# Eleven of the 22 groups of a feed-forward block's down projection by Strassen's seven products, five of them with sums of weights formed earlier and kept in DRAM

## The chip, the cores and the metric

The kernel runs on one core of one Trainium2 chip. The metric is the device time of one execution, in microseconds. Before the change three runs gave 1447.15, 1447.38 and 1447.71 us; the median is 1447.38.

## What is computed

One layer of a streaming encoder over 256 frames of 2048 channels, in float32: two token mixers side by side, their merge, then a feed-forward block with a short convolution on its gate half, and a last RMSNorm. The change lies in the feed-forward block:

```python
D_MODEL = 2048; SEQ = 256; D_FF = 5632; CONV_WIDTH = 3

def conv_glu(h, w_up, conv_w, conv_b, w_down):
    ug = h @ w_up
    gate, up = ug[..., :D_FF], ug[..., D_FF:]
    gate = lax.conv_general_dilated(
        gate, conv_w[:, None, :].astype(gate.dtype), window_strides=(1,),
        padding=((CONV_WIDTH - 1, 0),), dimension_numbers=('NWC', 'WIO', 'NWC'),
        feature_group_count=D_FF) + conv_b
    return (jax.nn.silu(gate) * up) @ w_down

def reference(...):
    ...
    h = h + conv_glu(rmsnorm(h, norm_ffn[l]), w_up[l], conv_w[l], conv_b[l], w_down[l])
    return rmsnorm(h, norm_final)
```

## The kernel before

**Products.** Every operand of a large product is split in two fp32r parts, `hi` (ScalarE copies, L96) and `lo` (VectorE subtracts, L97). `mm3` (L103) makes one product of three matmuls: activations 128 x 128 as the stationary operand, weights of up to 512 columns as the moving one, ah*bh, al*bh and ah*bl.

**Up projection** (loop over j, L910, 44 steps). A step loads two tiles of `w_up`, 1 MB each (`load_split`, L109), splits them, runs 32 matmuls of 512 columns (`wide`, L919) and 32 of 256 (`narrow`, L927), and then VectorE and ScalarE apply the norm, the convolution and SiLU (L940 to L954). The result is stored split in the units `ah` and `al`: as plain operands, or, for groups in `STRASSEN`, as three blocks of activations and four sums of blocks (`sums`, L353).

**Down projection** (`down_pair`, L1079). The 2048 output columns come in two pairs of 512-column blocks, p = 0 and 1 (1024 columns each), one after the other. In each, the 5632 rows of `w_down` are walked in 22 groups of 256 rows: one 1 MB load holds the four 128 x 512 blocks b21, b11, b12, b22 of a group. Four PSUM banks (`final`) collect the results.

- A plain group: two `pieces` of 1024 columns are split; 8 products, 24 matmuls.
- A Strassen group (`seven`, L312, and `strassen`, L330): VectorE forms b12 - b11 and b22 - b12 in `t13`, a unit buffer (L317), then b22 - t1 (L319) and b21 - that (L324); 3 1/2 splits of 1024 columns; 7 products, 21 matmuls. Four of the seven go into four more banks (`shared`), which after the last Strassen group are added to `h` (`h_steps`, L464).

**Order and buffers.** A planner puts each engine's instructions in order from the program's order, dependencies and free buffers. `weights_first` lets loads and splits of weights go 128 instructions ahead, `results_first` 64. Loads of weights are issued from SyncE's queue. There are three `raw` buffers of 1 MB (`wraw`), four `hi` and four `lo` buffers of 1024 columns (`wsplit`; the last quarter product's `four` takes a `hi`), and 18 units of 2048 columns. In the down projection 14 units hold `ah` and `al` and two hold `h`; the gains of the last norm take one at the last Strassen group (`load_gains`, L979) until the last multiply of `residual` (L1007).

**End.** For the last three groups of p = 1 the products of the second row block are held back, so that the first row block's norm and output (`residual`, `root`, `finish`) run beside them; `last_block` (L1051) makes the last product in two halves. `ordered` keeps these instructions in the written order.

## Time and profile before

| | before |
|---|---|
| median of three runs | 1447.38 us |
| the profiled execution | 1447.6 us |
| its span, first to last instruction | 1445.8 us |
| TensorE busy | 1435.6 us (99%) |
| VectorE busy | 1215.2 us (84%) |
| ScalarE busy | 807.3 us (56%) |
| read from HBM, written | 285.82 MB, 4.19 MB |

In the rows below times are in microseconds from the start of the span. PE is TensorE, PEld its weight loads, DVE VectorE, ACT ScalarE; an engine's name with a q behind it is its sequencer, which issues DMAs. L97 is line 97. `lo<-raw,hi` is the tile written and the tiles read. A row of the timeline has start, duration, engine, line, operation, tiles, shape and count, and in brackets how long the engine stood idle before it and what ended that. Matmuls overlap: their rows say 0.39 us, their starts lie closer.

### The profile page before, as it was taken

What the parts mean: (1) busy time and instruction counts of PE and PEld (TensorE: products, weight loads), DVE (VectorE), ACT (ScalarE), POOL (GpSimd) and SP (SyncE); (2) the same over time, 40 slices, a digit from 0 to 9 for tenths busy, and PEclk for the clock granted to TensorE, in tenths of its full rate; (3) what the DMA queues carried; (4) which work ended last, traced back from release to release, by engine and by line L of the source; (5) the groups of instructions that cost most, each with busy time, mean ns of one, the idle gap of its engine ahead of it and who ended that gap; (6) DMA issues with size and microseconds to landing.
All of it is one profiled execution on the core that took longest, in us unless ns stands there. A gap on an engine that the chain in (4) does not pass through costs nothing.

```text
span 1445.8 us, 18735 instructions
## 1 busy us (share of the span) xinstructions
PE 1435.6 (99%) x7138; PEld 1216.7 (84%) x7138; DVE 1215.2 (84%) x1706; ACT 807.3 (56%) x1042; POOL 0.2 (0%) x4
## 2 busy tenths in 40 slices
PE   9999999999999999999999999999999999999997
PEld 7888888888888888888888888888888888888886
DVE  6888998889888898999977787777777778988987
ACT  6655655566656554555655455544554555556553
POOL 0000000000000000000000000000000000000000
PEclk9999999999999999999999999999999999999999
DMA  9554455456455556555665455445544556565653
GB/s 380 199 209 175 168 193 214 175 200 229 146 204 196 211 193 215 213 194 204 236 216 188 175 190 208 185 175 192 208 183 175 192 207 237 209 218 187 221 211 124
DMA packets 43145, 291.22 MB, mean 201 GB/s; under 512 B 4912, under 2 KB 5808, under 8 KB 9008
## 3 DMA queue, kind: packets, MB, share of 16 engines
q1 hardware_dynamic: 42480, 288.99, 55.3%
q8 instruction: 56, 0.92, 0.3%
q10 hardware_dynamic: 576, 1.05, 0.2%
q14 instruction: 33, 0.27, 0.0%
HBM read 285.82 MB, written 4.19 MB: 201 GB/s over the span
## 4 chain that ended last, share of the span: by engine, by line
PE 94%; DVE 3%; DMA 1%; ACT 1%; issue 0%; DVEq 0%; ACTq 0%
PE acc L919 22%; PE acc L104 14%; PE acc L105 14%; PE acc L106 14%; PE acc L927 12%; PE aux L104 5%; PE aux L105 5%; PE aux L106 5%; DMA raw<-in_w_down 1%; DVE lo L97 1%; DVE u L97 1%; PE acc L425 0%; ACT hi L96 0%; PE aux L192 0%; DVE u L317 0%
## 5 line engine op out<-in xcount | busy, mean ns | idle before, releaser
L96 ACT ACTIVATE hi<-raw 128x1024 fp32r<-128x1024 f32 (+1 forms) x518 | 542.8, 1055 | 383.9 <-PE acc L105 165.9
L97 DVE TENSOR_TENSOR lo<-raw,hi 128x1024 fp32r<-128x1024 f32 (+1 forms) x518 | 613.9, 1216 | 118.1 <-ACT hi L96 65.0
L104 PE MATMUL acc<-hi,u 128*128 128x512 f32 x884 | 345.5, 391 | 0.1
L105 PE MATMUL acc<-hi,u 128*128 128x512 f32 x884 | 344.4, 390 | 0.0
L106 PE MATMUL acc<-lo,u 128*128 128x512 f32 x884 | 344.1, 389 | 0.0
L919 PE MATMUL acc<-u,hi 128*128 128x512 f32 x1408 | 328.3, 390 | 0.0
L919 PEld LDWEIGHTS acc<-u,hi 128*128 128x128 f32 x1408 | 261.3, 188 | 52.6 <-DVE u L101 0.2
L106 PEld LDWEIGHTS acc<-lo,u 128*128 128x128 f32 x884 | 165.9, 188 | 34.7 <-DVE lo L97 0.2
L104 PEld LDWEIGHTS acc<-hi,u 128*128 128x128 f32 x884 | 166.0, 188 | 34.3 <-DVE t L364 0.5
L105 PEld LDWEIGHTS acc<-hi,u 128*128 128x128 f32 x884 | 166.1, 188 | 33.4
L927 PEld LDWEIGHTS acc<-u,lo 128*128 128x128 f32 x1408 | 174.9, 192 | 3.5
L927 PE MATMUL acc<-u,lo 128*128 128x256 f32 x1408 | 176.0, 283 | 0.0
L104 PE MATMUL aux<-hi,u 128*128 128x512 f32 x268 | 104.6, 390 | 0.0
L106 PE MATMUL aux<-lo,u 128*128 128x512 f32 x268 | 104.4, 390 | 0.0
L105 PE MATMUL aux<-hi,u 128*128 128x512 f32 x268 | 104.3, 389 | 0.0
L942 ACT ACTIVATE t<-acc 128x256 f32<-128x256 f32 x88 | 33.8, 384 | 99.4 <-PE acc L927 99.4
L96 ACT ACTIVATE four<-raw 128x512 fp32r<-128x512 f32 x51 | 32.2, 632 | 66.0 <-DVE raw L324 33.1
L96 ACT ACTIVATE u<-u 128x1024 fp32r<-128x1024 f32 x53 | 55.7, 1055 | 23.0 <-DVE u L317 18.3
L317 DVE TENSOR_TENSOR u<-raw 128x1024 f32<-128x1024 f32 x51 | 62.1, 1218 | 6.4 <-DMA raw<-in_w_down 5.9
L97 DVE TENSOR_TENSOR u<-u,u 128x1024 fp32r<-128x1024 f32 x53 | 64.6, 1218 | 2.5 <-ACT u L96 2.5
L106 PEld LDWEIGHTS aux<-lo,u 128*128 128x128 f32 x268 | 50.3, 188 | 11.0 <-DVE lo L97 0.4
L104 PEld LDWEIGHTS aux<-hi,u 128*128 128x128 f32 x268 | 50.3, 188 | 10.3 <-ACT hi L96 0.2
(215 smaller groups left out, 1187.8 us busy)
## 6 DMA issues: line engine op xcount, KB each, us to landing
raw<-in_w_up SPq DMA_DIRECT2D x88, 1024.0 KB, 5.7
raw<-in_w_in SPq DMA_DIRECT2D x85, 1024.0 KB, 4.8
raw<-in_w_down SPq DMA_DIRECT2D x44, 1024.0 KB, 4.9
raw<-in_w_ret_proj SPq DMA_DIRECT2D x16, 1024.0 KB, 4.9
raw<-in_w_out SPq DMA_DIRECT2D x16, 1024.0 KB, 5.0
raw<-in_w_pool_proj SPq DMA_DIRECT2D x8, 1024.0 KB, 4.9
u<-in_x SPq DMA_DIRECT2D x4, 1024.0 KB, 9.3
raw<-in_w_early SPq DMA_DIRECT2D x4, 512.0 KB, 7.6
```

The source lines that it names most:

```text
L96: act.activation(hi, src, AF.Copy)
L97: dve.tensor_tensor(lo, src, plain(hi), ALU.subtract)
L104: pe.matmul(o, ah, bh, start=start, stop=False)
L105: pe.matmul(o, al, bh, start=False, stop=False)
L106: pe.matmul(o, ah, bl, start=False, stop=stop)
L317: dve.tensor_tensor(t13, raw[:, 2 * NB :], raw[:, NB : 3 * NB], ALU.subtract)
L919: pe.matmul(o[half], w2[half][hf][0][:, i * P : (i + 1) * P], hview(kt), start=kt == 0, stop=False)
L927: pe.matmul(o[half][:, :T], wl, hview(kt)[:, :T], start=False, stop=kt == KT - 1)
L942: act.activation(small_part[:, half * T : (half + 1) * T], o[half][:, T:], AF.Copy)
```

## The change

Eleven groups of each pair become Strassen groups in place of nine. Nine of them are formed during the up projection as before (`STRASSEN`, now at other places); for two more, `LATE`, the activations stay plain and their four sums are formed by `form_late` ahead of the down projection, in a unit of their own. For five groups, `PRE`, `prepare` loads the weights during the up projection, every third step, forms the sums in the `raw` buffer and stores it to DRAM through ScalarE's queue; the down projection then loads three blocks (0.75 MB, `w_down3`) and the sums (1 MB). The other six form the sums in place, without `t13`, after their own blocks have been split. At the end, `residual`'s add goes ahead by `results_first`, and the mean of the second row block is taken in `last_block`.

```diff
--- before.py
+++ after.py
@@ -31,7 +31,9 @@
 GN_EPS = 1e-5
 UNIT = 2048
 WARM = 9
-STRASSEN = (2, 4, 6, 8, 10, 12, 14, 16, 18)
+STRASSEN = (1, 3, 5, 7, 9, 12, 13, 15, 18)
+LATE = (10, 16)
+PRE = (1, 5, 10, 13, 16)
 STRASSEN_Z = (1, 3, 4, 5)
 STRASSEN_R = (0, 1, 3, 5)
 STRASSEN_O = (2, 3, 5)
@@ -297,6 +299,21 @@
         raw = load_raw(src)
         return [pieces(raw[:, i * 1024 : (i + 1) * 1024]) for i in range(2)]
 
+    def weight_sums(raw):
+
+        b = [raw[:, i * NB : (i + 1) * NB] for i in range(4)]
+        dve.tensor_tensor(raw[:, NB : 3 * NB], raw[:, 2 * NB :], raw[:, NB : 3 * NB], ALU.subtract)
+        dve.tensor_tensor(b[3], b[3], b[1], ALU.subtract)
+        dve.tensor_tensor(b[0], b[0], b[3], ALU.subtract)
+
+    def split_sums(raw):
+
+        q3, q2 = pieces(raw[:, 2 * NB :])
+        both = unit(F32R)
+        split(both[:, : 2 * NB], both[:, 2 * NB :], raw[:, : 2 * NB])
+        q4, q1 = ((both[:, i * NB : (i + 1) * NB], both[:, (2 + i) * NB : (3 + i) * NB]) for i in range(2))
+        return q2, q3, q1, q4
+
     class Pair:
 
 
@@ -327,8 +344,22 @@
             split(*q4, b21)
             return q11, q21, q2, q22, q3, q1, q4
 
-        def strassen(self, src, a, last):
-            q11, q21, q2, q22, q3, q1, q4 = self.seven(src)
+        @staticmethod
+        @weights_first
+        def seven_in_place(src):
+
+            raw = load_raw(src)
+            b = [raw[:, i * NB : (i + 1) * NB] for i in range(4)]
+            q21, q11 = pieces(raw[:, : 2 * NB])
+            four = wsplit.tile([P, 1024], F32R, tag="hi", name=nm("four"))
+            q22 = (four[:, :NB], four[:, NB:])
+            split(*q22, b[3])
+            weight_sums(raw)
+            q2, q3, q1, q4 = split_sums(raw)
+            return q11, q21, q2, q22, q3, q1, q4
+
+        def strassen(self, seven, a, last):
+            q11, q21, q2, q22, q3, q1, q4 = seven
             a11, a12, a22, s1, s2, s3, s4 = a
             p2, p3, p4, _ = self.final
             p1, p5, p6, p7 = self.shared
@@ -410,7 +441,7 @@
                     pair.shared = [(spare or aux_tile)() for _ in range(4)]
                 t0, t1 = slice(0, P), slice(P, T)
                 a = [a_of(g, 0, t0), a_of(g, 1, t0), a_of(g, 1, t1), *zs[g]]
-                pair.strassen(src(g), a, g == groups[-1])
+                pair.strassen(pair.seven(src(g)), a, g == groups[-1])
                 if g == groups[-1]:
                     todo.extend(steps(*pair.shared))
             elif ready and not g:
@@ -906,8 +937,33 @@
         o = n % 2 * 7 * P
         return [x[n // 2][:, o + c.start : o + c.stop] for x in (ah, al)]
 
+
+    sums_out = {
+        (p, g): tc.dram_tile([P, 4 * NB], F32, name=f"sums_out{p}_{g}") for p in range(2) for g in PRE
+    }
+
+    def prepare(p, g):
+        raw = load_raw(ins["w_down"][p * (NFF // 2) + g])
+        weight_sums(raw)
+        act.dma_start(sums_out[p, g], raw)
+
+    @weights_first
+    def seven_prepared(p, g):
+        ra = wraw.tile([P, 2048], F32, tag="raw", name=nm("raw"))
+        sp.dma_start(ra[:, : 3 * NB], ins["w_down3"][p * len(PRE) + PRE.index(g)])
+        rt = load_raw(sums_out[p, g])
+        q21, q11 = pieces(ra[:, : 2 * NB])
+        four = wsplit.tile([P, 1024], F32R, tag="hi", name=nm("four"))
+        q22 = (four[:, :NB], four[:, NB:])
+        split(*q22, ra[:, 2 * NB : 3 * NB])
+        q2, q3, q1, q4 = split_sums(rt)
+        return q11, q21, q2, q22, q3, q1, q4
+
+    todo_sums = deque(sums_out)
     cs = None
     for j in range(NFF):
+        if j % 3 == 2 and todo_sums:
+            prepare(*todo_sums.popleft())
 
         o = [acc_tile() for _ in range(2)]
         w2 = [load_split(ins["w_up"][2 * j + half]) for half in range(2)]
@@ -994,7 +1050,8 @@
         a = None
         for c in range(0, NB, n):
             s = slice(nb * NB + c, nb * NB + c + n)
-            seq(dve.tensor_tensor(h[tb][:, s], ps[:, c : c + n], h[tb][:, s], ALU.add))
+            with results_first():
+                seq(dve.tensor_tensor(h[tb][:, s], ps[:, c : c + n], h[tb][:, s], ALU.add))
             junk = t2k()
             i = nb + c // n
             seq(act.activation(junk[:, :n], h[tb][:, s], AF.Square, accum_out=ssq3[:, tb, i : i + 1]))
@@ -1005,11 +1062,15 @@
                 a = small.tile([P, 1], F32, tag="fin0", name=nm("fin"))
                 seq(dve.tensor_scalar(a, ssq3[:, tb, 3:4], 1.0 / D, part[:, tb : tb + 1], ALU.mult, ALU.add))
             seq(dve.tensor_tensor(g[:, c : c + n], h[tb][:, s], gf[:, c : c + n], ALU.mult))
-        if nb == 2:
-            pt = part[:, tb : tb + 1]
-            seq(dve.tensor_reduce(pt, ssq3[:, tb, :3], mybir.AxisListType.X, ALU.add))
-            seq(dve.tensor_scalar(pt, pt, 1.0 / D, RMS_EPS, ALU.mult, ALU.add))
+        if nb == 2 and tb == 0:
+            mean(tb)
         return a
+
+    def mean(tb):
+
+        pt = part[:, tb : tb + 1]
+        seq(dve.tensor_reduce(pt, ssq3[:, tb, :3], mybir.AxisListType.X, ALU.add))
+        seq(dve.tensor_scalar(pt, pt, 1.0 / D, RMS_EPS, ALU.mult, ALU.add))
 
     def root(tb, a):
 
@@ -1061,6 +1122,7 @@
         for i, x in enumerate(extra):
             seq(dve.tensor_tensor(hb[:, c[i]], x[:, :n], hb[:, c[i]], ALU.add))
             seq(act.activation(t2k(n), hb[:, c[i]], AF.Square, accum_out=ssq3[:, 1, 3 + i : 4 + i]))
+        mean(1)
         a = small.tile([P, 1], F32, tag="fin0", name=nm("fin"))
         seq(dve.tensor_scalar(a, ssq3[:, 1, 3:4], 1.0 / D, part[:, 1:2], ALU.mult, ALU.add))
         seq(dve.tensor_tensor(scaled[0][:, NB : NB + n], hb[:, c[0]], gf[:, :n], ALU.mult))
@@ -1075,6 +1137,22 @@
         for i in range(2):
             s = slice(i * 1024, (i + 1) * 1024)
             split(hi[:, s], lo[:, s], raw[:, s])
+
+    late = {}
+
+    def form_late():
+
+        room = unit(F32R)
+        for i, g in enumerate(LATE):
+            f = t2k()
+            dst = [room[:, (2 * i + j) * NB : (2 * i + j + 1) * NB] for j in range(2)]
+            for k in range(2):
+                dve.tensor_tensor(f[:, k * T : (k + 1) * T], *map(plain, plain_a(g, k, slice(0, T))), ALU.add)
+            a11, a21, a12, a22 = (f[:, j * P : (j + 1) * P] for j in range(4))
+            sums(a11, a12, a21, a22, dst)
+            late[g] = [[x[:, j * P : (j + 1) * P] for x in dst] for j in range(4)]
+
+    form_late()
 
     def down_pair(p, final, shared):
         pair = Pair(final)
@@ -1085,9 +1163,13 @@
             if g > STRASSEN[-1] + 1:
                 for _ in range(min(5, len(steps))):
                     steps.popleft()()
-            if g in STRASSEN:
-                a = [sums_a(g, slice(i * P, (i + 1) * P)) for i in range(7)]
-                pair.strassen(src, a, g == STRASSEN[-1])
+            if g in STRASSEN or g in LATE:
+                if g in STRASSEN:
+                    a = [sums_a(g, slice(i * P, (i + 1) * P)) for i in range(7)]
+                else:
+                    a = [plain_a(g, k, slice(tb * P, (tb + 1) * P)) for k, tb in ((0, 0), (1, 0), (1, 1))] + late[g]
+                seven = seven_prepared(p, g) if g in PRE else pair.seven_in_place(src)
+                pair.strassen(seven, a, g == STRASSEN[-1])
                 if g == STRASSEN[-1]:
                     load_gains(p)
                     steps.extend(h_steps(h, p)(*shared))
@@ -1169,6 +1251,8 @@
     a["w_ret_proj"] = _pairs(np.asarray(w_ret_proj)[0], np)
     a["w_out"] = _pairs(np.asarray(w_out)[0], np)
     a["w_down"] = _pairs(np.asarray(w_down)[0], np)
+    w = a["w_down"].reshape(2, NFF // 2, P, 4, NB)[:, PRE]
+    a["w_down3"] = w[:, :, :, [0, 1, 3]].reshape(-1, P, 3 * NB)
     up = np.asarray(w_up)[0].reshape(KT, P, 2, NFF, P).transpose(3, 2, 1, 0, 4)
     a["w_up"] = np.ascontiguousarray(up).reshape(2 * NFF, P, KT * P)
     g = np.asarray(w_pool_group)[0].reshape(4, 2, P, 256).transpose(2, 0, 1, 3)
```

## Rows read from the trace of the kernel before

In rows 1 the columns are the stretch and its length; then busy time and count of PE, PEld, DVE, ACT and POOL; the granted clock (1.00 is 2.4 GHz), the DMA engines' busy share and GB/s. In rows 8 they are count, busy time in us, mean in ns, idle time before and what ended it.

**Rows 1.** Busy time of each engine by stage: up projection, first pair, second pair.
```profile
731.00:1209.00 478.00, 478.00 (x2755) 423.35 (x2754) 363.63 (x564) 249.46 (x346) 0.00 (x0) 1.00 0.52 188
1209.00:1322.00 113.00, 113.00 (x502) 93.57 (x501) 100.86 (x108) 61.99 (x67) 0.00 (x0) 1.00 0.64 230
1322.00:1437.00 115.00, 115.00 (x512) 94.95 (x510) 102.10 (x124) 63.69 (x78) 0.00 (x0) 1.00 0.52 185
```

**Rows 2.** Timeline of VectorE, two groups of the first pair.
```profile
1258.94 0.69 DVE L97 TENSOR_TENSOR four<-raw,four 128x512 fp32r<-128x512 f32 x1 [0.15 <-ACT four L96]
...
1266.02 0.69 DVE L324 TENSOR_TENSOR raw<-raw 128x512 f32<-128x512 f32 x1
1266.63 1.22 DVE L97 TENSOR_TENSOR u<-u,u 128x1024 fp32r<-128x1024 f32 x1
1267.77 1.22 DVE L97 TENSOR_TENSOR lo<-raw,hi 128x1024 fp32r<-128x1024 f32 x1
1269.14 0.69 DVE L97 TENSOR_TENSOR four<-raw,four 128x512 fp32r<-128x512 f32 x1 [0.15 <-ACT four L96]
```

**Rows 3.** Timeline of TensorE, first product of group 10.
```profile
1260.97 0.39 PE L104 MATMUL aux<-hi,u 128*128 128x512 f32 x1
```

**Rows 4.** Chain that ended last, 1374 to 1424: start, duration, what.
```profile
1379.21 4.94 DMA raw<-in_w_down
...
1389.56 6.30 DMA raw<-in_w_down
...
1401.27 4.94 DMA raw<-in_w_down
```

**Rows 5.** Timeline of TensorE's weight loads, group 20 of the second pair.
```profile
1424.86 0.19 PEld L106 LDWEIGHTS aux<-lo,u 128*128 128x128 f32 x1 [0.42 <-DVE lo L97]
```

**Rows 6.** DMA issues: tiles, queue, count, KB each, median us to landing.
```profile
raw<-in_w_up SPq DMA_DIRECT2D x88, 1024.0 KB, 5.7
...
raw<-in_w_down SPq DMA_DIRECT2D x44, 1024.0 KB, 4.9
...
h_out<-u SPq DMA_DIRECT2D x2, 1024.0 KB, 6.8
```

**Rows 7.** Timeline of the up projection, TensorE's wide parts and ScalarE between them.
```profile
864.75 7.44 PE L919 MATMUL acc<-u,hi 128*128 128x512 f32 x32
...
875.87 7.44 PE L919 MATMUL acc<-u,hi 128*128 128x512 f32 x32
...
866.84 1.06 ACT L96 ACTIVATE hi<-raw 128x1024 fp32r<-128x1024 f32 x1 [1.50 <-PE acc L919]
```

**Rows 8.** Groups by line and shape, from 980 us: a 256-column VectorE operation.
```profile
L957 DVE TENSOR_TENSOR t<-t,t 128x256 f32<-128x256 f32 x14 | 6.0, 425 | 8.7 <-ACT t L954 8.7
```

**Rows 9.** Timeline at the turn of the pairs, TensorE and VectorE.
```profile
1322.89 0.39 PE L104 MATMUL aux<-hi,u 128*128 128x512 f32 x1
...
1330.81 0.69 DVE L1007 TENSOR_TENSOR u<-u,u 128x512 f32<-128x512 f32 x1
1333.02 1.23 DVE L97 TENSOR_TENSOR u<-u,u 128x1024 fp32r<-128x1024 f32 x1 [1.52 <-ACT u L96]
```

**Rows 10.** Timeline of VectorE at the end, second row block.
```profile
1435.37 0.69 DVE L1007 TENSOR_TENSOR u<-u,u 128x512 f32<-128x512 f32 x1
1436.12 0.15 DVE L1010 TENSOR_REDUCE part<-ssq 128x1 f32<-128x3 f32 x1
...
1436.38 0.68 DVE L1060 TENSOR_TENSOR u<-aux,u 128x512 f32<-128x512 f32 x1
```

**Rows 11.** Timeline from group 18 of the second pair on, VectorE and TensorE.
```profile
1414.51 0.68 DVE L97 TENSOR_TENSOR four<-raw,four 128x512 fp32r<-128x512 f32 x1
...
1415.37 0.40 PE L104 MATMUL acc<-hi,a_front 128*128 128x512 f32 x1
...
1416.49 1.23 DVE L97 TENSOR_TENSOR lo<-raw,hi 128x1024 fp32r<-128x1024 f32 x1 [1.29 <-ACT hi L96]
...
1421.31 2.36 DVE L97 TENSOR_TENSOR u<-raw,u 128x1024 fp32r<-128x1024 f32 x2 [0.73 <-ACT u L96]
```

## The prediction

> **What bounds the kernel now.** I read the page's totals, then the table by stage [rows 1]: TensorE is busy in all of the up projection (731 to 1209 us), of the first column pair (1209 to 1322) and of the second (1322 to 1437), at a granted clock of 1.00, the 2.4 GHz level. In the two pairs VectorE works 100.9 of 113 us and 102.1 of 115 us; in the up projection 363.6 of 478. So TensorE bounds the down projection and VectorE is close behind it.
>
> A steady stretch shows how close [rows 2]. VectorE's `four` of group 10 and that of group 12 start 10.20 us apart: one plain and one Strassen group, 24 + 21 = 45 matmuls, so 0.2267 us each and 5.44 and 4.76 us for the groups. Back-to-back starts give VectorE's pitch: 1.14 us for 1024 columns, 0.61 for 512. A plain group costs it 2 x 1.14 = 2.28, a Strassen group 4 x 1.14 + 3 x 0.61 = 6.39, together 8.7 of 10.2. Group 10's `four` is done at 1259.63; group 10 starts on TensorE at 1260.97 [rows 3] and uses those weights 18 matmuls later: a lead of over 5 us.
>
> The end tells more than the totals. The chain that ended last leaves TensorE at 1375 and runs through buffers [rows 4]: a load into one of three `raw` buffers (4.94 us), VectorE's sums and splits, the next load. The loads on it begin at 1379.21, 1389.56 and 1401.27: 10.35 and 11.71 us apart, against TensorE's 10.20. One load took 6.30 us, and the lead shrank until TensorE stood 0.42 us at 1424.86 for a `lo` of group 20 [rows 5], the only such wait that the timeline of the down projection has. A matmul taken out is therefore worth its time only while this loop of buffers keeps up.
>
> **The change part by part.**
>
> Products: eleven Strassen groups a pair instead of nine. Each drops 3 matmuls of 24; 2 x 2 x 3 = 12 x 0.2267 = **-2.72 us**. All are on TensorE's path, if the weights come in time.
>
> The Trainium skill, TensorE: Matmul & The Clock Gate, Back-to-back issue gap, gives 131 ns for a sustained 512-column matmul. By it the saving would be an estimated 1.57 us; the rows' 226.7 ns decide.
>
> Work moved to the up projection: ten times (two pairs, five groups) a 1 MB load, three sums of 1.14 + 0.61 + 0.61 = 2.36 us on VectorE, a 1 MB store from ScalarE's queue. VectorE has 114 us idle there [rows 1] for 23.6 us. What it can hurt is a `raw` buffer: load about 6 us, sums 2 to 4, store 6.8 (the store of `h_out`) [rows 6], some 16 us of one buffer in three, which is more than a step of the loop (875.87 - 864.75 = 11.12) [rows 7]. But the weights are early: `hi` of a later step is written at 866.84 to 867.90 and first used when the wide matmuls begin at 875.87, 8 us of lead in every step. A load that slips by 9 us, one round of a buffer, begins to show. ScalarE's queue stands at the store's issue until the last sum is done (behind it the next `hi`, with the same 8 us); SyncE's queue has the extra load between two weight loads. Value: 0; bounds 0 and 10 x 1 us.
>
> Prepared groups (1, 5, 10, 13, 16) in the down projection: no sums, 3 x 1.14 + 0.61 = 4.03 us of VectorE, but 1.75 MB in two `raw` buffers. Groups formed in place (3, 7, 9, 12, 15, 18): the same 6.39 us, but differently ordered. Now the sum into `t13` needs no split buffer and runs ahead; in place, q11, q21 and q22 must be split first, since the sums overwrite their blocks. The third `hi` buffer of such a group comes free in the middle of the plain group before it, 2.72 us ahead; with ScalarE's 1.06 us [rows 7] and VectorE's 1.14 the lead of q2 is about 2 us, where it is now 4.
>
> VectorE's total falls: 11 x 2.28 + 6 x 6.39 + 5 x 4.03 = 83.6 us a pair, against 13 x 2.28 + 9 x 6.39 = 87.2. The buffers do not profit. Loads go 9, 10, 10, 11, 12, 13, 13, 14, 15, 16, 16, 17, 18 round three buffers, so 11 waits for group 9's buffer, 14 for 12's, 17 for 15's, and an in-place group holds its buffer to its last split. A round is: load 4.9 + `hi` 1.1 + plain splits 2.3 + in-place group 6.4 + about 0.5 of waiting for ScalarE = 15.2 us. TensorE needs 66 x 0.2267 = 14.96 for the same three groups. With a load of 6.3 us, as the chain shows when two follow closely, it is 16.6. Three rounds lose 0.7 to 4.9 us against a lead of 2: a stall of **0 to 2.9 us a pair**. I take 0.7, which is a mean load of 5.6 us, between the median of 4.9 [rows 6] and the slow one: **+1.4**.
>
> The unit buffers: 14 for the activations, two for `h`, and one now for the late sums leave one of 18, where there were two. At the turn of the pairs the gains of pair 0 sit in it until the last multiply with them, at 1330.81 to 1331.50; only then could `both` be written (it was, at 1333.02) [rows 9]. Pair 1 starts at 1322.89; its first Strassen group was number 2 and is now number 1, which needs `both` after 24 + 15 matmuls, 8.8 us, at 1331.7. Same times as now would stall it some 1.7 us (1331.50 + 1.06 + 1.22 against 1331.7 + 0.45, when the first `lo` is due). But results now go ahead of weights, and VectorE has 2.4 us less to do there (4.03 for 6.39). **+0.3**, bounds 0 and 1.7.
>
> Late sums: for each of two groups six small operations of at most 0.43 us [rows 8] and one of 0.69, at most 6.5 us on VectorE near the start of pair 0, due only at group 10. Groups 1, 3, 5 in place of 2, 4, 6 save most of it (two at 4.03 for two at 6.39). Value 0.
>
> Tail: `mean` for the second row block moves behind the last adds. L1010, which waits for ScalarE's square, starts at 1436.12 and holds L1060 to 1436.38; the multiply of 1435.37 would have let it go at 1435.98 [rows 10]: **-0.4**, as far as TensorE's last matmuls permit. Against that VectorE, which now ends group 18 at 1415.19, before TensorE begins it, will end it 2 to 4 us after that begin (q1 is due 17 matmuls in, 3.9 us, with 0 to 2 us of lead), and its remaining work has two idle spells of 1.29 and 0.73 us to take this up [rows 11]: **+0.2**, bounds 0 and 1.8.
>
> Sum: -2.72 + 1.4 + 0.3 - 0.4 + 0.2 = **-1.2 us**. The profiled execution took 1447.6, of which 1445.8 are span; that gives 1446.4 for it. The median of the runs is 0.2 below it: **1446.2 us**.
>
> **The rivals.**
>
> A, all of it is hidden: the loop keeps up, as it does now through pair 0, and most of the wait of 0.42 us at 1424.86 goes too: -2.72 - 0.4 - 0.3 = -3.4, 1444.0. For it: VectorE has 3.6 us less to do in each pair. Against: 15.2 us a round leave nothing for one slow load.
>
> B, the tail sets the end and the matmuls count for nothing: the chain already runs past TensorE from 1375 on, and whatever TensorE gains before, VectorE's work after group 18 ends when it does: 1447.4 +- 0.7.
>
> C, slower: the same buffer loop with loads of 6.3 us, because a prepared group puts 1.75 MB on the engines at once. Stalls of 2.9 us in both pairs, and group 18's splits late by the full 1.8 in the tail: 5.8 + 1.8 - 3.1 = +4.5, 1451.9. It decides from a mean load of some 6.0 us on. For it: the 6.30 us in the chain. Against: the loads beside it took 4.94.
>
> D, slower too: the up projection shows the stores. A buffer held for over 20 us delays the next weights past their 8 us of lead, ten times by 1 us and more: -1.2 + 10 = +8.8, 1456. For it: all three buffers are in use there; against: 16 us by the rows.
>
> The Trainium skill, DMA: Bandwidth & Descriptors, Anatomy of one DMA, speaks for D: most of a DMA's fixed cost is the receipt of its last byte, which can be surprisingly long where HBM is written. By that rule, the trace agrees in direction (6.8 us to store 1 MB, 4.9 to load it [rows 6]).
>
> **How the numbers follow.** Forecast 0.45, A 0.27, B 0.15, C 0.09, D 0.04. 0.2% is 2.9 us, about what a measurement of this kernel can tell from no change. Faster: A and the low edge of the forecast, 0.29. Slower: C and D, 0.13. Same: 0.58. The range takes in A below, and above the forecast with 2 us a pair of stalls: 1443.7 to 1449.0.
>
> **What would show it.** TensorE without a wait in the up projection, 12 matmuls fewer, and waits of some tenths on `lo` or on `both` at groups 15 to 18 of each pair: the forecast. No such waits and an end near 1444: A. The same waits over a us, with landings of 6 us: C. Waits on L919: D. I am wrong in kind if group 1 of either pair waits by several us (the one unit buffer), or if the sums change nothing in the buffers' order.

## The result, and the profile after

The changed kernel is slower: 1459.68 us, median of 4 runs (1458.02 to 1462.71), against 1447.55 for the kernel before beside it; ratio 1.0085, 95% interval 1.0074 to 1.0097. The forecast of 1446.2 and its range up to 1449.0 are both missed. The profiled execution took 1462.71, the slowest of the four, of which 1460.9 are span; before, 1445.8.

The table by stage answers [rows 1], here cut at the first and last matmul of each stage: up projection, first pair, second pair, and the tail behind TensorE. The kernel before:

```profile
718.68:1209.26 490.58, 490.58 (x2831) 434.35 (x2830) 374.54 (x594) 258.98 (x366) 0.00 (x0) 1.00 0.53 192
1209.27:1322.90 113.63, 113.63 (x504) 94.04 (x503) 101.49 (x109) 61.99 (x67) 0.00 (x0) 1.00 0.64 232
1322.90:1437.04 114.14, 114.14 (x508) 94.21 (x506) 101.24 (x123) 63.69 (x78) 0.00 (x0) 1.00 0.51 183
1437.04:1445.81 8.77, 0.00 (x0) 0.00 (x0) 3.92 (x15) 1.92 (x6) 0.00 (x0) 0.79 0.38 133
```

The changed kernel, same stages:

```profile
718.66:1216.25 497.59, 492.92 (x2831) 434.22 (x2829) 392.57 (x625) 246.71 (x366) 0.00 (x0) 1.00 0.62 231
1216.26:1334.49 118.23, 114.97 (x497) 91.93 (x496) 99.74 (x118) 63.96 (x73) 0.00 (x0) 1.00 0.70 254
1334.49:1451.23 116.74, 114.26 (x502) 92.45 (x500) 96.88 (x114) 64.55 (x80) 0.00 (x0) 1.00 0.58 211
1451.23:1460.90 9.67, 0.00 (x1) 0.00 (x0) 5.38 (x18) 2.65 (x8) 0.00 (x0) 0.72 0.51 187
```

TensorE, busy in every microsecond of the first three stages before, now has gaps in all of them. The up projection is 7.0 us longer. The pairs should each have lost 6 x 0.2267 = 1.36 us and grew by 4.6 and 2.6: waits of 6.0 and 4.0 us. The tail grew by 0.9. 7.0 + 6.0 + 4.0 + 0.9 - 2.7 = 15.2; the two spans are 15.1 apart.

**The up projection.** Of the waits there, ScalarE's for loads of `w_up` were 3.1 us in all before (five times, 0.8 at most). After, first ScalarE's, then SyncE's queue:

```profile
ACT hi L98 <- DMA raw<-in_w_up: 79.8, 26, 8.1
...
SPq L114 <- DMA sums_out<-raw: 74.0, 9, 9.5
```

(us in total, times, longest.) The queue that loads weights stands behind the stores of the sums. One preparation of the ten (L288 loads the raw row, L305 to L307 are the three sums, L948 the store, L114 loads `w_up`), from the timelines of SyncE, VectorE, ScalarE and TensorE:

```profile
928.77 0.33 SPq L288 DMA_DIRECT2D raw<-in_w_down  x1
934.65 1.23 DVE L305 TENSOR_TENSOR raw<-raw 128x1024 f32<-128x1024 f32 x1 [0.23 <-DMA raw<-in_w_down]
935.79 4.63 DVE L99 TENSOR_TENSOR lo<-raw,hi 128x1024 fp32r<-128x1024 f32 x4
941.00 0.68 DVE L306 TENSOR_TENSOR raw<-raw 128x512 f32<-128x512 f32 x1
942.20 0.68 DVE L307 TENSOR_TENSOR raw<-raw 128x512 f32<-128x512 f32 x1
942.92 0.33 ACTq L948 DMA_DIRECT2D sums_out<-raw  x1
943.37 2.01 ACT L98 ACTIVATE hi<-raw 128x1024 fp32r<-128x1024 f32 x2 [7.91 <-DMA raw<-in_w_up]
944.47 3.93 PE L975 MATMUL acc<-u,hi 128*128 128x512 f32 x16 [1.34 <-ACT hi L98]
948.99 2.37 PE L975 MATMUL acc<-u,hi 128*128 128x512 f32 x9 [0.58 <-ACT hi L98]
```

and its two transfers, with the time to landing last:

```profile
raw<-in_w_down SPq DMA_DIRECT2D x1, 1024.0 KB, 5.9
sums_out<-raw ACTq DMA_DIRECT2D x1, 1024.0 KB, 7.3
```

5.9 us of load, 8.2 until the last sum is done (four splits of weights stand between the first and the second), 7.3 of store: the buffer is held for 21.4 us, and TensorE waits 1.34 + 0.58.

The other nine holds are of the same kind, 20.0 to 22.5 us each, but they don't all cost the same. TensorE's waits of over 0.3 us stand behind three of the ten preparations only (at 943 and 948, 1012 and 1017, 1047 and 1052 us); behind the first four there is none at all. The early holds are covered by the lead of the weights; why the eighth costs nothing either stays open.

**The down projection.** One round of two Strassen groups and a plain one, groups 14 to 16 of the first pair. 14 is plain, 15 formed in place, 16 prepared (L953 loads its plain blocks). SyncE's queue, then ScalarE, VectorE, and SyncE's queue again:

```profile
1282.62 2.07 SPq L288 DMA_DIRECT2D raw<-in_w_down  x2
1286.93 0.33 SPq L953 DMA_DIRECT2D raw<-in_w_down  x1
1291.49 0.33 SPq L288 DMA_DIRECT2D raw<-sums_out  x1
...
1288.01 2.01 ACT L98 ACTIVATE hi<-raw 128x1024 fp32r<-128x1024 f32 x2 [2.37 <-DMA raw<-in_w_down]
1291.94 1.06 ACT L98 ACTIVATE hi<-raw 128x1024 fp32r<-128x1024 f32 x1 [1.93 <-DMA raw<-in_w_down]
...
1289.10 2.36 DVE L99 TENSOR_TENSOR lo<-raw,hi 128x1024 fp32r<-128x1024 f32 x2 [2.20 <-ACT hi L98]
1293.04 1.23 DVE L99 TENSOR_TENSOR lo<-raw,hi 128x1024 fp32r<-128x1024 f32 x1 [1.58 <-ACT hi L98]
1294.78 1.22 DVE L305 TENSOR_TENSOR raw<-raw 128x1024 f32<-128x1024 f32 x1
1296.04 0.69 DVE L306 TENSOR_TENSOR raw<-raw 128x512 f32<-128x512 f32 x1
1296.76 0.69 DVE L307 TENSOR_TENSOR raw<-raw 128x512 f32<-128x512 f32 x1
1297.93 1.22 DVE L99 TENSOR_TENSOR lo<-raw,hi 128x1024 fp32r<-128x1024 f32 x1 [0.48 <-ACT hi L98]
1299.08 1.22 DVE L99 TENSOR_TENSOR u<-raw,u 128x1024 fp32r<-128x1024 f32 x1
...
1300.32 19.95 SPq L288 DMA_DIRECT2D raw<-in_w_down  x6
```

Group 14's load at 1282.62 waited for group 12's buffer, group 17's at 1300.32 for group 15's, whose last read ends at 1300.30: a round of 17.70 us, for 14.96 of TensorE. It is: load of 14, 5.4 (first ScalarE copy 1288.01); copy 1.1; two splits 2.36; 1.58 idle, because 15's own load took 7.5; 7.26 for group 15. The rounds that start at 1265.64 and, in the second pair, at 1381.89 and 1399.31 take 17.0, 17.4 and 17.4. VectorE, which works 99.7 of 118 us here, works 13.2 us of the 17.70 and stands still for 4.5, of which 2.20 and 1.58 are waits behind the loads of 14 and 15.

### The profile page after: what moved, and what is told of

Same layout as the page of the kernel before. It is cut to its first block, busy times and chain, and to the rows that moved or that the text cites. A ratio compares the mean times of both kernels' runs of the same rounds, so it can differ in the third digit from the quotient of the medians.

```text
span 1460.9 us, 18848 instructions
## 1 busy us (share of the span) xinstructions
PE 1439.4 (99%) x7126; PEld 1212.6 (83%) x7126; DVE 1228.5 (84%) x1740; ACT 798.6 (55%) x1052; POOL 0.2 (0%) x4
## 4 chain that ended last, share of the span: by engine, by line
PE 76%; DMA 10%; DVE 9%; ACT 3%; issue 2%; ACTq 0%; DVEq 0%; SPq 0%
PE acc L975 14%; PE acc L106 13%; PE acc L108 13%; PE acc L107 13%; PE acc L983 7%; DMA raw<-in_w_down 5%; DVE lo L99 5%; PE aux L106 5%; PE aux L107 4%; PE aux L108 4%; DMA raw<-in_w_up 3%; ACT hi L98 2%; DMA sums_out<-raw 1%; DVE u L99 1%; DVE raw L305 0%
## 5 line engine op out<-in xcount | busy, mean ns | idle before, releaser
L98 ACT ACTIVATE hi<-raw 128x1024 fp32r<-128x1024 f32 (+1 forms) x518 | 536.3, 1053 | 463.1 <-PE acc L107 146.2
L106 PE MATMUL aux<-hi,u 128*128 128x512 f32 x260 | 101.9, 392 | 1.6 <-ACT hi L98 1.6
L108 PE MATMUL aux<-lo,u 128*128 128x512 f32 x260 | 101.1, 391 | 0.3 <-DVE lo L99 0.3
L107 PE MATMUL aux<-hi,u 128*128 128x512 f32 x260 | 101.3, 389 | 0.0
L106 PEld LDWEIGHTS aux<-hi,u 128*128 128x128 f32 x260 | 48.8, 188 | 12.7 <-ACT hi L98 3.0
L107 PEld LDWEIGHTS aux<-hi,u 128*128 128x128 f32 x260 | 48.8, 188 | 9.9
L99 DVE TENSOR_TENSOR u<-t,u 128x256 fp32r<-128x256 f32 (+2 forms) x56 | 30.2, 546 | 26.9 <-ACT u L98 26.8
L998 ACT ACTIVATE t<-acc 128x256 f32<-128x256 f32 x88 | 30.2, 373 | 28.8 <-PE acc L983 28.8
L99 DVE TENSOR_TENSOR four<-raw,four 128x512 fp32r<-128x512 f32 x55 | 37.8, 687 | 9.3 <-ACT four L98 9.3
```

Source lines behind the costliest of these rows:

```text
L98: act.activation(hi, src, AF.Copy)
L99: dve.tensor_tensor(lo, src, plain(hi), ALU.subtract)
L106: pe.matmul(o, ah, bh, start=start, stop=False)
L107: pe.matmul(o, al, bh, start=False, stop=False)
L108: pe.matmul(o, ah, bl, start=False, stop=stop)
L998: act.activation(small_part[:, half * T : (half + 1) * T], o[half][:, T:], AF.Copy)
```

## The experiments

U is the theory that the loss in the up projection comes from the raw buffers held by the preparations; L, that the down projection's loss is its own. All lengths are from the profiled execution, read as above; the kernel before gave medians of 1447.38 to 1447.90 beside them.

| kernel | up | pair 0 | pair 1 | tail | median us | ratio, 95% interval |
|---|---|---|---|---|---|---|
| before | 490.58 | 113.63 | 114.14 | 8.77 | 1447.55 | |
| changed | 497.59 | 118.23 | 116.74 | 9.67 | 1459.68 | 1.0085 [1.0074, 1.0097] |
| up_only | 499.81 | 113.63 | 114.24 | 8.54 | 1455.83 | 1.0053 [1.0038, 1.0068] |
| down_only | 490.54 | 118.71 | 115.31 | 9.73 | 1455.03 | 1.0047 [1.0030, 1.0064] |
| sums_first | 517.17 | 119.00 | 116.25 | 9.65 | 1480.41 | 1.0226 [1.0211, 1.0241] |
| all_in_place | 490.56 | 119.65 | 115.53 | 9.80 | 1456.43 | 1.0058 [1.0043, 1.0073] |
| prep_in_units | 490.60 | 117.15 | 115.90 | 9.96 | 1455.42 | 1.0055 [1.0040, 1.0070] |
| in_place_nine | 490.58 | 113.63 | 113.83 | 8.29 | 1447.55 | 0.9998 [0.9989, 1.0007] |
| two_loads_nine | 490.58 | 113.63 | 113.83 | 9.28 | 1448.26 | 1.0003 [0.9994, 1.0012] |
| tail_only | 490.59 | 113.63 | 113.86 | 8.37 | 1447.54 | 0.9998 [0.9989, 1.0008] |
| one_load | 490.59 | 112.61 | 112.47 | 7.87 | 1444.51 | 0.9979 [0.9970, 0.9988] |
| one_load_bytes | 490.60 | 112.59 | 112.47 | 7.97 | 1444.19 | 0.9978 [0.9969, 0.9987] |
| no_sums_eleven | 490.55 | 112.61 | 112.47 | 8.38 | 1444.71 | 0.9980 [0.9971, 0.9990] |
| spread_eleven | 490.61 | 114.26 | 114.17 | 9.65 | 1449.55 | 1.0012 [1.0004, 1.0021] |
| ten | 490.60 | 113.37 | 113.87 | 8.38 | 1446.80 | 0.9995 [0.9986, 1.0004] |
| one_block | 490.54 | 116.75 | 112.87 | 9.73 | 1450.20 | 1.0019 [1.0010, 1.0028] |
| one_block_late | 490.61 | 117.85 | 112.76 | 8.05 | 1450.27 | 1.0014 [1.0005, 1.0023] |
| one_block_six | 490.60 | 112.63 | 112.78 | 9.01 | 1445.37 | 0.9986 [0.9977, 0.9995] |

### Which half of the change

up_only adds the ten preparations to the kernel before:

```diff
+        if j % 3 == 2 and todo_sums:
+            prepare(*todo_sums.popleft())
```

> The kernel before with one thing added: the ten preparations during the up projection (load, three sums, store); nothing reads the stored sums, and the down projection is that of before with nine Strassen groups. Theory U (a raw buffer held from the load to the landing of the store, with SyncE's queue standing behind it): the up projection grows from 490.6 by 5 to 9 us, the two pairs stay at 113.6 and 114.1, total +5 to +9 us. Rival (the preparations are hidden by the 8 us of lead, as predicted, and the up projection of the changed kernel suffers from its other order of groups): total within 0.7 us of before.

down_only takes them out of the changed kernel, and so leaves out the sums of the five prepared groups:

```diff
-        rt = load_raw(sums_out[p, g])
+        rt = load_raw(ins["w_down"][p * (NFF // 2) + g])
...
-        if j % 3 == 2 and todo_sums:
-            prepare(*todo_sums.popleft())
```

> The changed kernel without the preparations; the five prepared groups load their 1 MB of sums as unsummed rows of the weights, so the forming of their sums is left out, while every load, split and product of the down projection stays. Theory U plus L (U for the up projection; L: in the down projection the loop of three raw buffers is too slow for groups that load 1.75 MB): the up projection is back at 490.6 +- 0.5, the pairs stay near 118 and 117, total about 7 us under the changed kernel and 4 to 6 us over before. Rival (the down projection is late only because it inherits a late start of its weights from the up projection): the pairs fall under 114 us each, total 1 to 3 us under before.

The halves come apart cleanly: up_only is late in the up projection alone, down_only in the pairs and the tail alone. Two losses, neither inherited from the other. Their sizes don't add up as neatly: 7.9 and 7.1 us in the medians make 15.0, where the changed kernel lost 12.1 (15.1 in its profiled execution), and down_only came out 7.1 us above the kernel before, where 4 to 6 was expected.

### The up projection: which part of the hold

```diff
-        weight_sums(raw)
-        act.dma_start(sums_out[p, g], raw)
+        with tc.high_priority(offset=256):
+            weight_sums(raw)
+            act.dma_start(sums_out[p, g], raw)
```

> The changed kernel with the three sums and the store of each preparation given a higher priority than the weights of the up projection, nothing else. In the changed kernel the sums wait some 8 us after the load has landed. Theory U: the hold of the raw buffer falls from 21 us to 15, TensorE's waits in the up projection go almost wholly, the up projection takes 490.6 to 492.5, total 5 to 7 us under the changed kernel. Rival (the up projection waits because 21 MB more share the DMA engines): still 495 to 499 us.

Theory U's expectation fell, and the rival's too: the up projection takes 517.17 us, 25 more than U allowed. VectorE's sums now stand ahead of splits and wait for their load, and ScalarE's longest wait for `w_up` grows to 10.9 us; from the timelines of VectorE and ScalarE, and the waits:

```profile
874.79 1.23 DVE L305 TENSOR_TENSOR raw<-raw 128x1024 f32<-128x1024 f32 x1 [0.84 <-DMA raw<-in_w_down]
...
885.56 2.01 ACT L98 ACTIVATE hi<-raw 128x1024 fp32r<-128x1024 f32 x2 [10.85 <-DMA raw<-in_w_up]
...
ACT hi L98 <- DMA raw<-in_w_up: 110.3, 28, 10.9
```

The sums' part of the hold did shrink, from 8.2 us to 4.7 (874.79 to 879.48), but the hold did not: the stores, now beside loads of `w_up`, land later. Over the up projection, the changed kernel first, then sums_first:

```profile
sums_out<-raw ACTq DMA_DIRECT2D x10, 1024.0 KB, 6.9
...
sums_out<-raw ACTq DMA_DIRECT2D x10, 1024.0 KB, 9.6
```

The hold shown here runs from a load issued at 867.70 to a landing at 889.14, 21.4 us again. Ten such holds cost 26.6 us of up projection here and 7.0 in the changed kernel. So this run did not test a shorter hold, but it shows that the length of the hold doesn't set the loss alone. It fits the trace that the sums now delay the splits that free the other two buffers; no run tests that by itself. The loss isn't one stretch, then; it may be a fourth user on three buffers. prep_in_units takes the preparations off them:

```diff
-        raw = load_raw(ins["w_down"][p * (NFF // 2) + g])
+        raw = unit()
+        sp.dma_start(raw, ins["w_down"][p * (NFF // 2) + g])
```

> The changed kernel, but each of the ten preparations loads, sums and stores in a buffer of 2048 columns that stands free during the up projection, so that the three raw buffers serve only the weights of the up projection. Everything else, the down projection with it, is the changed kernel's. Theory B (a raw buffer held over 21 us is what delays the up projection's weights): the up projection goes back to 490.6 to 491.5 us from 497.6, the pairs stay at 118 and 116, the total is some 7 us under the changed kernel's, 1452 to 1453. Rival B2 (what delays them is the 21 MB more that the DMA engines move beside them, or the sums in VectorE's order): the up projection stays at 495 to 499 us and the total at 1457 to 1460.

```profile
718.62:1209.22 490.60, 490.60 (x2831) 434.38 (x2829) 394.35 (x625) 256.76 (x366) 0.00 (x0) 1.00 0.63 234
```

TensorE has no gap left in the up projection, with the same sums on VectorE (394.35 us busy, 392.57 in the changed kernel) and the same bytes (234 GB/s, 231). Theory B holds: the buffer, not the bytes or VectorE. The total, 1455.42, came out some 3 us above what was expected, though still 4.3 under the changed kernel's; the changed kernel's profiled execution, from which the 7 us were taken, is its slowest.

### The down projection: order, loads, places

all_in_place sets `PRE = ()`: no preparation, eleven groups in place.

> The changed kernel with all eleven Strassen groups formed in place, no preparation and no prepared group. Up projection 490.6. Loads are 1 MB a group, but VectorE needs 6.39 + 6.39 + 2.28 = 15.1 us for two Strassen and one plain group, TensorE 15.0. Theory L (the 1.75 MB in two of three buffers make the waits): pairs of 112.5 to 115 us, total 1 us under to 2 us over before. Rival (it is the order in place, sums after splits, that makes the waits): pairs of 117 us and more, total 5 us and more over before.

Its pairs are as late as the changed kernel's, without a 1.75 MB load. Its VectorE timeline has, from group 12 on, the sums of groups 12, 13, 15 and 16 (S S P S S):

```profile
1273.23 1.22 DVE L305 TENSOR_TENSOR raw<-raw 128x1024 f32<-128x1024 f32 x1
...
1280.40 1.22 DVE L305 TENSOR_TENSOR raw<-raw 128x1024 f32<-128x1024 f32 x1
...
1289.83 1.22 DVE L305 TENSOR_TENSOR raw<-raw 128x1024 f32<-128x1024 f32 x1
...
1297.01 1.22 DVE L305 TENSOR_TENSOR raw<-raw 128x1024 f32<-128x1024 f32 x1
```

In place after in place 7.17 us, with a plain group between 9.43: a round of 16.60 us of VectorE without a pause worth naming. The in-place group costs it 7.17, not 6.39, because its three sums follow from one another and the next split waits 0.48 us for ScalarE, which waits for L306. That isn't all of pair 0's loss: some 3.0 us of it lie before 1243 us, at groups 2 to 5, where plain and Strassen groups alternate (one_block below waits at the same place). Three runs take the conditions one at a time. in_place_nine forms the nine groups of the kernel before in place, at the old places:

```diff
-                pair.strassen(src, a, g == STRASSEN[-1])
+                pair.strassen(pair.seven_in_place(src), a, g == STRASSEN[-1])
```

> The kernel before with its nine Strassen groups at the same alternating places (2, 4, ... 18), but each formed in place as the changed kernel forms six of its eleven: q11, q21 and q22 split first, then the sums over the raw blocks, then q2, q3, q1, q4. No preparation, no load of 1.75 MB. What the prediction counted on (a lead of some 2 us is enough): pairs of 113.6 and 114.1 us as before, total within 0.5 us of 1447.5. Rival (the order in place costs TensorE time whatever the places are): pairs 2 us and more longer each, total 1451 and more.

two_loads_nine keeps the old places and gives groups 2, 6, 10, 14 and 18 the two loads (it leaves their sums out, so VectorE has less to do than before):

```diff
+        sp.dma_start(ra[:, : 3 * NB], src[:, : 3 * NB])
+        rt = load_raw(src)
```

> The kernel before, but in each pair its groups 2, 6, 10, 14 and 18 load 0.75 MB and 1 MB into two raw buffers and form no sums, as prepared groups do (the sums of their weights are left out; the second load is the plain row). Places, the other groups and the up projection are those of before. Theory (1.75 MB in two of three buffers are what makes the loop of buffers late): pairs of 116 us and more against 113.6, total 1451 and more, although VectorE has 12 us less to do in each pair. Rival (the two loads are carried at alternating places, and the loop is late from the order in place or from Strassen groups that follow one another): pairs at 113.6 or a little less, total 1446 to 1448.

Where plain and Strassen groups alternate, neither costs anything that can be told from nothing. no_sums_eleven is all_in_place without the line `weight_sums(raw)`:

> all_in_place (eleven groups formed in place, one load each, no preparation) with the three sums of the weights left out. Theory V (in all_in_place VectorE itself sets the round of two Strassen groups and a plain one: its in-place group takes 7.17 us from row to row, not the predicted 6.39, so 2 x 7.17 + 2.28 = 16.62 us against TensorE's 14.96, and the trace's rounds are 16.61): without the sums a group costs it some 4.1 us, and the pairs go from 119.65 and 115.53 to 112.2 to 112.6 us, total 1443.5 to 1445. Rival (adjacent Strassen groups, or eleven of them, are late through the four split buffers): pairs of 114 us and more, total 1448 and more.

one_load is prep_in_units with one load for a prepared group, which leaves its plain blocks out:

```diff
-        sp.dma_start(ra[:, : 3 * NB], ins["w_down3"][p * len(PRE) + PRE.index(g)])
-        rt = load_raw(sums_out[p, g])
+        rt = ra = load_raw(sums_out[p, g])
```

> prep_in_units, but a prepared group reads only the 1 MB of its sums, into one raw buffer, and takes its three plain blocks from there too (the 0.75 MB of plain blocks are left out). VectorE's work, the order of the groups and the up projection are those of prep_in_units. Theory F (a round of two Strassen groups and a plain one makes four loads into three buffers when one of the two is prepared, so one buffer has to carry two loads, 5.05 + 3.5 + 7.0 + 1.8 = 17.4 us, against TensorE's 14.96): with three loads in three buffers the pairs fall from 117.15 and 115.90 to 112.2 to 113 us, total 1447 or less. Rival (two Strassen groups in a row are late whatever is loaded): pairs 115 us and more, total 1451 and more.

Both bring the pairs to 112.6 and 112.5, the whole saving, with eleven groups at the changed kernel's places. So in one_load adjacent Strassen groups are carried, with one buffer a group and, by an estimate, 13.5 us of VectorE a round (7.17 in place, 2.28 plain, and the prediction's 4.03 prepared). (The sum in that text, 5.05 + 3.5 + 7.0 + 1.8, follows the wrong buffer: the round is the one shown above, through the in-place group.) Two things left together there, bytes and a buffer; one_load_bytes moves the 0.75 MB all the same:

```diff
+        sp.dma_start(beside[p, g], ins["w_down3"][p * len(PRE) + PRE.index(g)])
```

> one_load (a prepared group reads only its 1 MB of sums into one raw buffer and takes its plain blocks from there, which leaves the plain blocks out), but the 0.75 MB that it leaves out are moved all the same, from DRAM to DRAM, on the same queue and at the same place, and hold no raw buffer. Theory F1 (a buffer too few: four loads through three buffers): pairs of 112.5 to 113 us as in one_load, total 1444 to 1446. Rival F2 (bytes: loads beside others land after 7 us and more): pairs of 115 us and more as in prep_in_units (117.15, 115.90), total 1450 and more.

```profile
1209.03:1321.62 112.59, 112.56 (x497) 92.86 (x496) 100.67 (x118) 65.29 (x73) 0.00 (x0) 1.00 0.64 234
...
raw<-in_w_down SPq DMA_DIRECT2D x1, 1024.0 KB, 7.2
```

The pair is as short as without the bytes, though a load beside them still lands after 7.2 us (issued at 1264.35). Theory F1 holds: four loads through three buffers, not slow loads, break the round.

### Versions

tail_only, the change's last part alone:

> The kernel before with only the change's last part: the adds of the residual go ahead in VectorE's order and the mean of the second row block stands behind the last adds. The prediction's own term: -0.4 us on the tail of 8.77 us, total 1447.1. Rival (the tail of 9.67 us that the changed kernel shows comes from this part, not from VectorE's late splits of group 18): the tail grows to 9.5 us and more, total 1448.3.

The tail is 0.4 us shorter, as the prediction had it, and the total 0.1 in the median, which can't be told from nothing. Nor is the 0.4 shown to be this part's: in_place_nine, which leaves the tail's code as it was, has 8.29. It isn't what lengthened the tail of the changed kernel.

spread_eleven and ten form all groups in place, the late sums from group 5 on, and move the adjacent ones apart:

```diff
-STRASSEN, LATE = (1, 3, 5, 7, 9, 12, 13, 15, 18), (10, 16)
+STRASSEN, LATE = (1, 3, 4, 6, 8, 10, 13, 15, 18), (11, 17)   # spread_eleven
+STRASSEN, LATE = (1, 3, 5, 7, 9, 12, 14, 16, 18), (10,)      # ten
```

> Eleven groups in place with one load each, as all_in_place, but with the three places where two Strassen groups follow one another moved apart: 1, 3, 4, 6, 8, 10, 11, 13, 15, 17, 18 instead of 9-10, 12-13, 15-16; the late sums are formed from group 5 on. By theory V each such place costs 16.62 - 14.96 = 1.65 us of lead and each alternating pair of groups gives back 10.20 - 9.45 = 0.75: with a lead of 2 us most of it is absorbed, the pairs are 112.2 to 113.5 us, and the tail grows by the lateness of group 18, up to 1.65 us: total 1445.0 to 1448. Rival (the number of eleven is what costs, not the places): pairs of 115 us and more, total 1451 and more.

> Ten groups in place with one load each: 1, 3, 5, 7, 9, 10, 12, 14, 16, 18, one place (9-10) where two Strassen groups follow one another, the late sums of group 10 formed from group 5 on, no preparation. Theory V: 6 matmuls fewer than the kernel before (a stall from the one place of 1.65 us at most 0 to 0.5 beyond the lead), pairs of 112.9 to 113.4 us, total 1446.0 to 1447.2. Rival (the start at group 1 or the late sums cost as much as is saved): total 1447.6 and more.

spread_eleven cuts the waits of the two pairs to a third and no more: 228.4 us for both, against 235.2 in all_in_place and 225.1 without waits. Its pairs of 114.2 lie above the expected 113.5, and its adjacent places in pair 0 still cost 0.5 to 0.7 us each (starts of matmuls at 1232, 1268 and 1304): the lead is not regained in two alternating pairs of groups as reckoned. ten's total comes out within its expectation, though not its pair 1 (113.87 for 113.4 at most), and can't be told from the kernel before.

one_block makes a prepared group fit one buffer. Only X = b22 - b12 + b11 is formed ahead and stored, 0.25 MB; X - b11, b21 - X and b22 - X then don't wait for one another:

```diff
-        rt = load_raw(sums_out[p, g])
...
+        sp.dma_start(raw[:, : 3 * NB], ins["w_down3"][p * len(PRE) + PRE.index(g)])
+        sp.dma_start(raw[:, 3 * NB :], sums_out[p, g])
...
+        dve.tensor_tensor(b11, x, b11, ALU.subtract)
+        dve.tensor_tensor(b21, b21, x, ALU.subtract)
...
+        dve.tensor_tensor(b22, b22, x, ALU.subtract)
```

> The changed kernel's eleven groups at its places, nothing left out, but of a prepared group only one block of 0.25 MB is formed in the up projection, in a free buffer instead of a raw one (b22 - b12 + b11: 2 x 0.61 us of VectorE, a store of 0.25 MB), for the groups 9, 10, 12, 13, 15 and 16. In the down projection such a group loads 0.75 + 0.25 MB into one raw buffer and forms the other three sums by three independent operations of 0.61 us: 4 x 1.14 + ... = 3 x 1.14 + 4 x 0.61 = 5.86 us of VectorE, against 7.17 in place. A round of two such groups and a plain one is 2 x 5.86 + 2.28 = 14.0 us of VectorE and three buffers, against TensorE's 14.96. Theory (F1 and V): up projection 490.6 us, pairs 112.2 to 112.8, total 1444 to 1445.5, under the kernel before by 2 to 3.5 us. Rival (places are late anyway, or the twelve preparations show): pairs 114 and more, or up projection 492 and more; total 1447 and more.

Half right: pair 1 is 112.87, pair 0 116.75, with some 3.4 us of its waits in the first 33 us, where VectorE also forms the late sums. one_block_late forms these from group 5 on and prepares group 18 as well:

> one_block with two moves: the late sums of groups 10 and 16 are formed from group 5 of pair 0 on and not at its start, and group 18 is prepared too (14 preparations of one block), so that VectorE has 5.86 us and not 7.17 of it. Theory (late sums at the start cost one_block 2.9 us in pair 0, and VectorE's work on group 18 sets the tail): pair 0 goes from 116.75 to 112.3 to 112.9 us, pair 1 stays at 112.5 to 112.9, the tail goes from 9.73 to 8.4 to 9.1 us: total 1444.5 to 1446. Rival (groups 1 and 3 in place are what pair 0's start does not carry; the tail has another cause): pair 0 stays above 115, the tail at 9.7, total 1449 to 1450.

The tail fell further than expected, to 8.05; pair 0 did not fall. Its last two preparations found a free buffer only at the start of pair 0, beside the loads of `h`, and ScalarE then waited for their store; SyncE's queue, then ScalarE:

```profile
1208.69 0.81 SPq L947 DMA_DIRECT2D u<-in_w_down  x2
...
1210.43 0.93 SPq L1039 DMA_DIRECT2D u<-h_out  x2
...
1223.01 1.06 ACT L98 ACTIVATE u<-raw 128x1024 fp32r<-128x1024 f32 x1 [2.50 <-DMA sums_out<-u]
```

one_block_six goes back to twelve preparations:

```diff
-PRE = (9, 10, 12, 13, 15, 16, 18)
+PRE = (10, 12, 13, 15, 16, 18)
```

> one_block_late with group 9 formed in place again: twelve preparations of one block (10, 12, 13, 15, 16, 18 of both pairs), the late sums from group 5 on, group 18 prepared. Theory (the late sums at the start of pair 0 cost one_block 2.9 us; nothing else is left): pair 0 112.5 to 113.0 us, pair 1 112.6 to 112.9, tail 8.0 to 8.4, up projection 490.6: total 1444.7 to 1445.8, some 2.5 us under the kernel before. Rival (groups 1 and 3 in place are more than pair 0's start carries, whenever the late sums are formed): pair 0 above 114.5, total 1447 and more.

```profile
719.29:1209.89 490.60, 490.60 (x2831) 434.37 (x2830) 386.63 (x619) 258.38 (x366) 0.00 (x0) 1.00 0.60 217
1209.89:1322.52 112.63, 112.62 (x497) 92.77 (x496) 106.99 (x133) 63.79 (x73) 0.00 (x0) 1.00 0.64 233
1322.52:1435.31 112.79, 112.79 (x502) 93.04 (x500) 105.95 (x132) 65.21 (x82) 0.00 (x0) 1.00 0.52 186
1435.31:1444.32 9.01, 0.00 (x0) 0.00 (x0) 3.75 (x15) 1.99 (x6) 0.00 (x0) 0.78 0.35 123
```

1445.37 us, 2.2 under the kernel before and 14 under the changed one, with the same products. The interval excludes no change. Most of the rest was the late sums: pair 0 fell by 4.1 us from one_block, and the 3.4 us of waits at its start are gone. (Group 9, formed in place again, comes after those waits.) The tail of 9.01 is above the expected 8.4, and why one arrangement has 8.0 and another 9 stays open.

## Why the prediction was wrong

**The step that failed first: "Work moved to the up projection ... Value: 0".** The measured value is 7.0 us. That lies within the text's own bounds, 0 to 10; the step took the lower one. Its sum for a held buffer was 6 + 2 to 4 + 6.8, "some 16 us". Load and store were right (5.9, 7.3); the middle term was mis-sized: 8.2 us, since VectorE takes the three sums in its own order, between splits that come first. The real hold is 21.4 us. The text itself put the point of decision at "over 20 us" (rival D) and gave it 0.04. But the size of the hold isn't all of the failure: sums_first has the same hold and loses 26.6 us, and the changed kernel's ten like holds cost TensorE at three places. What had no price is that the weights' loads, splits and copies have to go round two buffers while the third is held. The lead of 8 us [rows 7] was read rightly, but the text counted on it "in every step", and it is used up. By the Trainium skill, DMA: Bandwidth & Descriptors, Anatomy of one DMA, told there for transfers that GpSimd issues, the receipt of a write to HBM can be long. The trace agrees in direction, with 7.3 us for this store and 5.9 for the load of the same size; no run shows how much of it is the receipt. And prep_in_units has the same ten stores and loses nothing: a long store costs only through the buffer it holds.

**The second: the round of 15.2 us in the down projection.** The chain was right, 14 for 12's buffer and 17 for 15's. Three things made it longer. The load took 5.4 for 4.9. A wait of 1.58 for the in-place group's own load, which is under way beside two others and takes 7.5, stood nowhere in the sum; its "about 0.5 of waiting for ScalarE" is another wait, and came true (0.48, within the 7.26). And the in-place group took 6.8 without that 0.48, for 6.4, since starts of independent operations [rows 2] were added up for sums that depend on each other. 17.70 instead of 15.2, and waits of 6.0 and 4.0 us where 0.7 a pair stood (its mean load of 5.6 us gives 0.8). Even the bound, 2.9, was too low, because it varied the load alone. The prediction's "0 to 2.9" asked how slow loads are; one_load_bytes shows that the question was how many share three buffers.

**C and D were called rivals and were not.** Their waits both came, in two stages, from one cause, three raw buffers with a user too many; the chances should not have been split between them. C's own reason did not come true: it put the stalls down to slow loads, and one_load_bytes has loads of 7.2 us without a stall.

**What held.** Products: with the waits gone (one_load, no_sums_eleven) the two pairs are 112.61 + 112.47 against 227.77, 2.69 us less for the 2.72 reckoned; in one_block_six, which leaves nothing out, they are 2.35 less. The turn of the pairs: pair 1 of the changed kernel has no wait before its group 12. The mean at the tail, -0.4, is what tail_only shows, but tails differ by as much without it. VectorE's end behind TensorE: the tail grew by 0.9, so 1.3 if the -0.4 is there, within "0 to 1.8" (VectorE works 5.38 us of the changed tail, 3.92 before); rival B's mechanism is there, but as a small term. Late sums at 0: about right where groups 1 and 5 are prepared, as in the changed kernel, and some 3.4 us in one_block, where groups 1 and 3 are formed in place beside them: the value depended on the cover, which the prediction did not price.

## What to carry to other kernels

A buffer ring is a resource like an engine: count its users per round, and for each the whole hold, with the place of its work in the other engines' order, before giving a moved transfer a price of nothing. Operations that depend on one another cost more than their pitches added up, and idle time of an engine on average does not say that it comes when a buffer waits. Work hoisted into a stage that one engine fills may find room on the other engines and in bandwidth, as here, and still cost that engine time through a buffer; a free buffer elsewhere, or a smaller thing to store, made the same hoist pay here.

## What the runs showed of the hardware

A wait can cost twice. In up_only TensorE waited 2.33 us for a load; the stretch before it, the wait, and the one behind it:

```profile
1012.00:1014.50 2.50, 2.50 (x23) 2.50 (x23) 2.50 (x5) 0.00 (x0) 0.00 (x0) 1.00 0.80 288
1014.50:1017.00 2.50, 0.37 (x4) 0.16 (x2) 2.33 (x5) 0.92 (x1) 0.00 (x0) 1.00 1.05 387
1017.00:1021.00 4.00, 3.81 (x10) 3.03 (x11) 2.36 (x2) 1.32 (x3) 0.00 (x0) 0.57 0.80 326
```

After it the granted clock was 0.57 over 4 us, near the 1.2 GHz level, and 10 matmuls ran where 17 would have. In one_block_late a wait of 2.32 us was followed by the same 0.57, with matmuls of 512 columns starting 0.43 us apart (1225.58, 1226.01, 1226.44) in place of 0.2267. Waits of up to 1.46 us in the changed kernel left the clock at 1.00. In sums_first a wait of 2.20 us (from 996.87) did so too, and one of 2.38 (from 1069.37) did not; the stretch behind each:

```profile
999.10:1003.00 3.90, 3.90 (x18) 3.22 (x19) 3.87 (x6) 2.71 (x5) 0.00 (x0) 1.00 1.02 433
...
1071.80:1075.80 4.00, 4.00 (x12) 3.21 (x13) 3.65 (x7) 2.32 (x4) 0.00 (x0) 0.66 1.02 428
```
